# A mixture-of-experts layer: first blocks of small experts in two passes, sums of halves under conditions, weight remainders on VectorE alone

## The chip, the cores and the metric

One core of one Trainium2 chip. The metric is the device time of one execution in microseconds (us). TensorE does the matmuls, ScalarE (ACT in the profile) and VectorE (DVE) work on what they leave in PSUM, GpSimd (POOL) issues gathers and scatters, SyncE (SP) issues the loads of weights. Each engine runs its own instructions strictly in the order in which they are written to it, and waits on semaphores for the others.

## The reference

One decoder layer over 2048 tokens of width 1024: four sequence mixers, a norm, then a hierarchical mixture of experts, and a second norm. The change is in the experts alone. Each token goes to 2 of 32 experts, which lie in 4 groups of 8:

```
group_p, group_idx = lax.top_k(softmax(xt @ w_rg + b_rg), 1)
e_logits = (xt @ w_re + b_re).reshape(t_tok, 4, 8)[its group]
expert_p, local_idx = lax.top_k(softmax(e_logits), 2)
gate = group_p * expert_p / sum(expert_p)
def expert_block(xb, e):                 # rows of one expert
    return (silu(xb @ w_gate[e]) * (xb @ w_up[e])) @ w_down[e]
y = segment_sum(y_rows * gate, token)
```

`w_gate` and `w_up` are 1024 x 512 for each expert, `w_down` is 512 x 1024, all in float32. How many rows an expert has is known only at run time: 4096 assignments fall on 32 experts.

## The kernel before

**Precision.** A float32 product is made of matmuls on high and low parts: `xh*wh + xh*wl + xl*wh`, three passes. The high part of a weight is a cast on ScalarE (`split_piece`, L1835), the low part is what the cast loses, a subtraction on VectorE or GpSimd (L1836). The weights of one expert come in six raw pieces of 1 MB (`m_raw`, 5 buffers): four for gate and up (`m_g`, 8 buffers, just the high and low parts of one expert), two for down (`m_dh`, `m_dl`). So there are 12 casts and 12 subtractions of 128 x 1024 for each expert. Of the subtractions 8 are VectorE's, and 4 are GpSimd's: the last gate/up piece and the last down piece.

**Blocks.** The rows of an expert are gathered in blocks of 128: block 0 always, block 1 if the count is over 128, block 2 (rare) if it is over 256, in `third`. A block of full form is three passes: 48 matmuls of 128 x 512 for gate and up (`moe_gu`, L1884, into the PSUM tiles `m_g0` for block 0 and `m_g1` for block 1; the trace calls both `m_g`, the instruction lists `m_g_18058` and `m_g_18059`) and 24 for down (`moe_dn`, L1916, into `m_y`, the one tile `yb` for both blocks). A block with at most 64 rows can be done in two passes: its transposed rows are laid out `spread`, so that the high parts of 64 rows and the low parts of the same rows fill one 128-wide operand (`passes`). That is 32 and 16 matmuls; the sums of the two halves must then be added. For gate and up `fold` does that (two ScalarE copies scaled by the 0/1 mask `m_half`, L1892, and two VectorE adds, L1893), for down a multiply-add in `moe_y` (L1925). Before the change only block 1 has this form: TensorE chooses it by a condition, the other engines do the fold and the multiply-add for every expert, scaled by 0 where nothing is to be added.

**One turn.** The 32 experts are done one after the other, in the order `ORDER`. In the turn of expert e the kernel does gate and up of e, the activation (`moe_h`: a tanh on ScalarE, L1900, and two VectorE steps, L1901 and L1902, for each block), turns the gathered rows of e + 1 (`turned`: TensorE transposes into `bank`, L1408, a ScalarE cast L51 and a VectorE subtraction L52 per bank of 4 transposes; two PSUM banks in all), does down of e - 1 (`down0`, then `down1`), turns the activations `m_t` of e into `m_h`, and splits the next weights. After each down come two ScalarE copies of `m_y` (`moe_y`, L1923), and a scatter-add (L1930) by GpSimd. `down1` writes the tile that the copies of `down0` read.

**What sets the order.** The calls in `moe()` are a program; a scheduler then orders each engine's instructions inside the stretches between conditions. A condition (`tc.If`) is a boundary: what is inside a branch stays together, and what is outside can't be put between its instructions. All blocks 0 are outside any condition before the change. `third` is a condition that four engines test once in each turn (L2011).

## Time and profile before

| | |
|---|---|
| median of 3 runs | 3057.15 us (3054.57 to 3073.09) |
| profiled execution, its own time | 3065.59 us |
| its span, first to last instruction | 3063.8 us |
| TensorE busy in the span | 2826.6 us (92%) |
| VectorE, ScalarE, GpSimd busy | 1934.6, 1225.6, 887.9 us |
| mean granted clock of TensorE | 0.946 of 2.4 GHz |

The span is the profiled execution alone; the median is of other executions of the same program. Busy times are sums over a program with quite different stages, so the stage of the experts, from about 1990 to 2935 us, has to be read by itself.

### The profile page before, as it was taken

What the parts mean: (1) busy time and instruction counts of PE and PEld (TensorE: products, weight loads), DVE (VectorE), ACT (ScalarE), POOL (GpSimd) and SP (SyncE); (2) the same over time, 40 slices, a digit from 0 to 9 for tenths busy, and PEclk for the clock granted to TensorE, in tenths of its full rate; (3) what the DMA queues carried; (4) which work ended last, traced back from release to release, by engine and by line L of the source; (5) the groups of instructions that cost most, each with busy time, mean ns of one, the idle gap of its engine ahead of it and who ended that gap; (6) DMA issues with size and microseconds to landing.
All of it is one profiled execution on the core that took longest, in us unless ns stands there. A gap on an engine that the chain in (4) does not pass through costs nothing. (4 is left out here: it accounts for less than half of the span.)

```text
span 3063.8 us, 42798 instructions
## 1 busy us (share of the span) xinstructions
PE 2826.6 (92%) x15420; PEld 2225.7 (73%) x15421; DVE 1934.6 (63%) x4061; ACT 1225.6 (40%) x2003; POOL 887.9 (29%) x552
## 2 busy tenths in 40 slices
PE   8999999999989999999999999898899888999866
PEld 6898877777867766665577799776677767777644
DVE  6366365366555567776646735677677866667868
ACT  4222132222124423333311112265576656566854
POOL 1000000011010023334431101445464544546524
PEclk9999999999989898989999999999999999999988
DMA  6332242121125422110243412377597767877865
GB/s 189 100 102 71 69 125 70 55 73 56 53 50 164 158 79 80 50 38 18 83 141 136 143 69 70 114 276 259 182 309 233 251 230 230 264 246 244 286 223 195
DMA packets 287042, 442.98 MB, mean 145 GB/s; under 512 B 84088, under 2 KB 152040, under 8 KB 286760
## 3 DMA queue, kind: packets, MB, share of 16 engines
q1 hardware_dynamic: 272200, 397.78, 39.2%
q0 software_dynamic: 14560, 41.47, 5.4%
q8 instruction: 172, 2.82, 0.4%
q14 instruction: 110, 0.90, 0.1%
HBM read 350.52 MB, written 96.50 MB: 146 GB/s over the span
## 5 line engine op out<-in xcount | busy, mean ns | idle before, releaser
L1884 PE MATMUL m_g<-m_g,xhl 128*128 128x512 f32 x2032 | 521.0, 404 | 16.4 <-PEq L2011 9.1
L1884 PEld LDWEIGHTS m_g<-m_g,xhl 128*128 128x128 f32 x2032 | 376.0, 192 | 110.1 <-issue 31.5
L1836 DVE TENSOR_TENSOR m_g<-m_raw,m_g 128x1024 fp32r<-128x1024 f32 x188 | 273.5, 1482 | 109.7 <-ACT m_g L1835 104.4
L1835 ACT CAST m_g<-m_raw 128x1024 fp32r<-128x1024 f32 x252 | 255.4, 1058 | 111.2 <-PEq L2011 99.2
L1916 PE MATMUL m_y<-m_dh,m_h 128*128 128x512 f32 x656 | 225.8, 409 | 24.0 <-PEq L2011 7.3
L59 PE MATMUL pbank<-xh,wh 128*128 128x512 f32 x544 | 226.6, 417 | 6.6 <-DVE us L213 3.6
L60 PE MATMUL pbank<-xl,wh 128*128 128x512 f32 x544 | 218.8, 402 | 0.0
L61 PE MATMUL pbank<-xh,wl 128*128 128x512 f32 x544 | 218.3, 402 | 0.0
L51 ACT CAST xhl<-bank 128x512 fp32r<-128x512 f32 x204 | 118.3, 609 | 240.2 <-PE bank L1408 239.1
L1836 POOL TENSOR_TENSOR m_g<-m_raw,m_g 128x1024 fp32r<-128x1024 f32 x64 | 184.9, 2971 | 84.5 <-ACT m_g L1835 47.5
L1466 PE MATMUL wide<-wt,xhl 128*128 128x512 f32 x768 | 183.2, 397 | 3.6 <-ACT xhl L51 3.6
L1836 POOL TENSOR_TENSOR m_dl<-m_raw,m_dh 128x1024 fp32r<-128x1024 f32 x64 | 178.3, 2819 | 23.9 <-ACT m_dh L1835 23.7
L1304 POOL TENSOR_TENSOR mla_acc<-mla_acc,mla_pt 128x512 f32<-128x512 f32 (+3 forms) x112 | 132.2, 1180 | 147.4 <-ACT mla_pt L1302 137.4
L1466 PEld LDWEIGHTS wide<-wt,xhl 128*128 128x128 f32 x768 | 143.9, 189 | 40.0 <-ACT xhl L51 7.5
L1302 ACT ACTIVATE mla_pt<-sbank 128x512 f32<-128x512 f32 (+3 forms) x160 | 85.3, 533 | 212.6 <-PE sbank L1298 110.8
L1916 PEld LDWEIGHTS m_y<-m_dh,m_h 128*128 128x128 f32 x656 | 128.6, 196 | 57.1 <-issue 10.8
L52 DVE TENSOR_TENSOR xhl<-bank,xhl 128x512 fp32r<-128x512 f32 x204 | 136.2, 684 | 49.9 <-ACT xhl L51 48.0
L1930 POOL DMA_INDIRECT accd<-m_y,m_put x47 | 96.1, 2044 | 247.2 <-ACT m_y L1923 148.1
L59 PE MATMUL pbank<-wh,xh 128*128 128x256 f32 x512 | 151.8, 296 | 0.0
L1646 PE MATMUL gate<-wt,xhl 128*128 128x354 f32 (+1 forms) x864 | 150.3, 331 | 1.1 <-ACT xhl L51 0.9
L60 PE MATMUL pbank<-wl,xh 128*128 128x256 f32 x512 | 150.3, 293 | 0.0
L61 PE MATMUL pbank<-wh,xl 128*128 128x256 f32 x512 | 149.1, 291 | 0.0
(643 smaller groups left out, 6279.6 us busy)
## 6 DMA issues: line engine op xcount, KB each, us to landing
m_raw<-in_moe_w_down SPq DMA_DIRECT2D x64, 1024.0 KB
m_raw<-in_moe_w_gate SPq DMA_DIRECT2D x126, 512.0 KB
m_raw<-in_moe_w_up SPq DMA_DIRECT2D x126, 512.0 KB
wraw<-in_w_in SPq DMA_DIRECT2D x80, 256.0 KB
o_x<-in_x SPq DMA_DIRECT2D x16, 512.0 KB
x1d<-m_g SPq DMA_DIRECT2D x16, 512.0 KB
accd<-wide SPq DMA_DIRECT2D x16, 512.0 KB
m_raw<-accd SPq DMA_DIRECT2D x7, 1024.0 KB
```

The source lines that it names most:

```text
L51: nc.scalar.copy(hi, src)
L52: (eng and nc.gpsimd or nc.vector).tensor_sub(lo, src, hi.bitcast(F32))
L59: nc.tensor.matmul(out, lh, rh, start=start, stop=False)
L60: nc.tensor.matmul(out, lh, rl, start=False, stop=False)
L61: nc.tensor.matmul(out, ll, rh, start=False, stop=stop)
L1304: (nc.vector if kt in self.SUMS else nc.gpsimd).tensor_add(acc[:, c0 * 128:512], acc[:, c0 * 128:512], pt[:, 0:n])
L1466: nc.tensor.matmul(p[:, j], a[:, k], W[k][bb][:, j * 512:j * 512 + 512], start=k == 0 and i == 0, stop=k == 7 and i == 2)
L1646: nc.tensor.matmul(p[:, 0:n], a[:, k], b[:, o:o + n], start=k == 0 and i == 0, stop=k == 7 and i == 2)
L1835: self.nc.scalar.copy(h[:, i], raw[:, i])
L1836: lo_eng.tensor_sub(l[:, i], raw[:, i], h[:, i].bitcast(F32))
L1884: self.mark["pe"] = self.nc.tensor.matmul(banks[:, j], a, b[:, k % 2, j * 512:j * 512 + 512], start=k == 0 and i == 0, stop=k == 7 and i = ...
L1916: self.nc.tensor.matmul(p[:, j], a, b[:, k % 2, j * 512:j * 512 + 512], start=k == 0 and i == 0, stop=k == 3 and i == len(ps) - 1)
```

## The change

First blocks get the form that second blocks had: their rows and activations are turned `spread` too, and TensorE tests whether the count is at most 64 (`sized(e, 0, ...)`), for gate/up and for down. The masked fold and the masked multiply-add of the down sums give way to a fold without a mask, inside a condition that ScalarE and VectorE test, for gate/up and down, for both blocks; the condition for block 1 is a pair, over 128 first and then at most 192. ScalarE and VectorE now load the counts into registers for it. The 4 subtractions of each expert that GpSimd did go to VectorE.

```diff
--- before.py
+++ after.py
@@ -1733,7 +1733,7 @@
             self.lists(lt)
             self.moe_gather(self.midx[:, 0:1], x0)
             embed(L + 2)
-            return G0, self.turned(x0)
+            return G0, self.turned(x0, spread=True)
 
     LATE = 4
 
@@ -1770,8 +1770,7 @@
         half, u = tl([128, n], F32, "m_half"), tl([128, n], F32, "m_mu")
         self.mhalf = half
         v = half.rearrange("p (e b) -> p b e", e=32)
-        nc.vector.memset(half, 1.0)
-        for b in range(1, self.NB):
+        for b in range(self.NB):
             nc.vector.tensor_scalar(v[:, b], self.base, 128.0 * b + 64, None, op0=OP.is_le)
 
         plain = tl([128, n], F32, "m_plain")
@@ -1884,12 +1883,15 @@
                     self.mark["pe"] = self.nc.tensor.matmul(banks[:, j], a, b[:, k % 2, j * 512:j * 512 + 512],
                                           start=k == 0 and i == 0, stop=k == 7 and i == len(ps) - 1)
 
-    def fold(self, p, m):
+    def fold(self, p, m=None):
 
         t = self.mw.tile([128, 512], F32, name="m_fold", bufs=1)
         for j in range(2):
             h = t[64 * j:64 * j + 64]
-            self.nc.scalar.activation(h, p[64:128, j], AF.Identity, scale=m[64:128])
+            if m is None:
+                self.nc.scalar.copy(h, p[64:128, j])
+            else:
+                self.nc.scalar.activation(h, p[64:128, j], AF.Identity, scale=m[64:128])
             self.nc.vector.tensor_add(p[0:64, j], p[0:64, j], h)
 
     def moe_h(self, banks, gate, t=None):
@@ -1964,11 +1966,11 @@
         def load_g(e):
             done = list(G0) if e == 0 else []
             R = [self.raw_gu(e, k) for k in range(len(done), 4)]
-            GW[e] = done + [self.split_piece((self.g_tile(), self.g_tile()), r, nc.gpsimd if i == len(R) - 1 else nc.vector) for i, r in enumerate(R)]
+            GW[e] = done + [self.split_piece((self.g_tile(), self.g_tile()), r, nc.vector) for r in R]
 
         def load_d(e):
             R = [self.raw_dn(e, k) for k in range(2)]
-            DW[e] = [self.split_piece(self.d_tiles(), r, g) for r, g in zip(R, (nc.vector, nc.gpsimd))]
+            DW[e] = [self.split_piece(self.d_tiles(), r, nc.vector) for r in R]
 
         def gather0(e):
             if e < experts:
@@ -1986,25 +1988,39 @@
                 self.moe_put(Y.pop(e), put(e, 1))
 
         def turn(e, b):
-            return self.moe_ht(H.pop((e, b)), spread=b > 0)
-
-        def sized(e, b, f):
-
-            with tc.If(cnt[e, "pe"] > 128 * b + 64) as c:
-                f(False)
-            with c.Else():
-                f(True)
+            return self.moe_ht(H.pop((e, b)), spread=True)
+
+        def sized(e, b, f=None, p=None):
+
+            def pe():
+                with tc.If(cnt[e, "pe"] > 128 * b + 64) as c:
+                    f(False)
+                with c.Else():
+                    f(True)
+
+            def add():
+                with tc.If(cnt[e, "two"] <= 128 * b + 64):
+                    self.fold(p)
+
+            g, n = (pe, "pe") if f else (add, "two")
+            if b:
+                with tc.If(cnt[e, n] > 128 * b):
+                    g()
+            else:
+                g()
 
         yb = self.yb
 
+        def down(e, b, h):
+            sized(e, b, lambda s: self.moe_dn(h, DW[e], yb, half=s))
+            sized(e, b, p=yb)
+            return self.moe_y(yb)
+
         def down0(e, h):
-            self.moe_dn(h, DW[e], yb)
-            self.moe_put(self.moe_y(yb), put(e, 0))
+            self.moe_put(down(e, 0, h), put(e, 0))
 
         def down1(e, h):
-            with tc.If(cnt[e, "pe"] > 128):
-                sized(e, 1, lambda s: self.moe_dn(h, DW[e], yb, half=s))
-            Y[e] = self.moe_y(yb, half(e, 1))
+            Y[e] = down(e, 1, h)
 
         def third(e):
 
@@ -2029,7 +2045,7 @@
 
         def counts(e):
             if e % 4 == 0:
-                for t, k, g in ((self.turn_cnt, "pe", [ET.PE]), (self.turn_cnt, "pool", [ET.Pool]), (self.turn_max, "four", FOUR)):
+                for t, k, g in ((self.turn_cnt, "pe", [ET.PE]), (self.turn_cnt, "pool", [ET.Pool]), (self.turn_cnt, "two", [ET.Activation, ET.DVE]), (self.turn_max, "four", FOUR)):
                     for i, v in enumerate(load_counts(t, e, g)):
                         cnt[e + i, k] = v
 
@@ -2038,7 +2054,7 @@
         if not x0:
             gather0(0)
         gather(0)
-        x0 = x0 or self.turned(X[0])
+        x0 = x0 or self.turned(X[0], spread=True)
         x1 = self.turned(X[1], spread=True)
         b0, b1 = self.gu
         ht = None
@@ -2049,14 +2065,13 @@
             third(e - 1)
             gather(e + 1)
             gather0(e + 1)
-            self.moe_gu(x0, GW[e], b0)
-            with tc.If(cnt[e, "pe"] > 128):
-                sized(e, 1, lambda s: self.moe_gu(x1, GW[e], b1, half=s))
-            H[e, 0] = self.moe_h(b0, gate(e, 0))
-            self.fold(b1, half(e, 1))
-            H[e, 1] = self.moe_h(b1, gate(e, 1))
+            sized(e, 0, lambda s: self.moe_gu(x0, GW[e], b0, half=s))
+            sized(e, 1, lambda s: self.moe_gu(x1, GW[e], b1, half=s))
+            for b, p in enumerate((b0, b1)):
+                sized(e, b, p=p)
+                H[e, b] = self.moe_h(p, gate(e, b))
             if e + 1 < experts:
-                x0 = self.turned(X[0])
+                x0 = self.turned(X[0], spread=True)
                 load_g(e + 1)
             if e == 31:
                 self.lx, self.lp, self.lt = {}, {}, {}
```

With the conditions the scheduler gives the engines another order. Three places, all in the turn of an expert in the middle of the stage; in brackets stand the semaphores that an instruction waits for, named by the engine that raises them.

TensorE, from the end of `down0` to the start of `down1`, before: `m_y<-` are the down matmuls, `m_t` the turning of the activations, `m_g_18058` gate and up of the next expert's block 0.

```order
L1916 MATMUL m_y<-m_dl,m_h 128x512
L1916 MATMUL m_y<-m_dh,m_h 128x512
L1408 MATMUL bank<-ident,m_t 128x128 [waits DVE_49]
L1408 MATMUL bank<-ident,m_t 128x128 x3
L1884 MATMUL m_g_18058<-m_g,xhl 128x512 [waits Activation_49]
L1884 MATMUL m_g_18058<-m_g,xhl 128x512 x4
L2005 COMPARE_AND_BRANCH
L1993 COMPARE_AND_BRANCH
L1916 MATMUL m_y<-m_dh,m_h 128x512 [waits Activation_49]
```

And in the changed kernel, where `xg_18064` is the turning of the next expert's rows of block 0:

```order
L1996 UNCONDITIONAL_BRANCH
L1408 MATMUL bank<-ident,m_xg_18064 128x128 [waits DMASW4_49,PE_49]
L1408 MATMUL bank<-ident,m_xg_18064 128x128 x3
L1408 MATMUL bank<-ident,m_xg_18064 128x128 [waits PE_49]
L1408 MATMUL bank<-ident,m_xg_18064 128x128 x3
L2002 UNCONDITIONAL_BRANCH
L2007 UNCONDITIONAL_BRANCH
L2002 UNCONDITIONAL_BRANCH
L2007 COMPARE_AND_BRANCH
L1996 COMPARE_AND_BRANCH
L1918 MATMUL m_y<-m_dh,m_h 128x512 [waits DVE_49,Activation_49]
```

Before, the rows of the next expert are turned at the start of `down0`, and `down0`, the first bank of `m_t` and five gate/up matmuls stand between that and `down1`; now the eight transposes of the rows come after `down0`, `down1` comes right behind them, then both banks of `m_t`, and the gate/up matmuls of the next expert in one piece behind those.

ScalarE, at the start of the same turn, before: `m_t<-m_g_18058` is the tanh of block 0, `xhl<-bank` the cast of the turned rows, `m_y<-m_y` the copies after `down0`.

```order
L1835 CAST m_g<-m_raw 128x1024 [waits DMAHW7_49,DMAHW0_49,PE_49]
L1900 ACTIVATE m_t<-m_g_18058 128x512
L1892 ACTIVATE m_fold<-m_g_18059,m_half 64x512 [waits DVE_49,Activation_49]
L51 CAST xhl<-bank 128x4x128 [waits PE_49] x2
L1835 CAST m_g<-m_raw 128x1024
L1892 ACTIVATE m_fold<-m_g_18059,m_half 64x512 [waits DVE_49]
L1835 CAST m_g<-m_raw 128x1024 [waits DMAHW2_49,DMAHW1_49]
L1835 CAST m_g<-m_raw 128x1024
L1900 ACTIVATE m_t<-m_g_18059 128x512 [waits DVE_49]
L1923 COPY m_y<-m_y 128x512 [waits DMASW5_49,PE_49]
L1923 COPY m_y<-m_y 128x512
```

And in the changed kernel, without the branches' bodies:

```order
L1834 CAST m_g<-m_raw 128x1024 [waits DMAHW7_49,DMAHW0_49,PE_49]
L1834 CAST m_g<-m_raw 128x1024
L51 CAST xhl<-bank 128x4x2x64 [waits DVE_49,PE_49,Activation_49]
L2002 COMPARE_AND_BRANCH
...
L2007 COMPARE_AND_BRANCH
...
L1902 ACTIVATE m_t<-m_g_18058 128x512 [waits DVE_49]
L1902 ACTIVATE m_t<-m_g_18059 128x512 [waits DVE_49]
L51 CAST xhl<-bank 128x4x2x64 [waits PE_49]
L1834 CAST m_g<-m_raw 128x1024 [waits DMAHW2_49,DMAHW1_49]
L1834 CAST m_g<-m_raw 128x1024
L2002 COMPARE_AND_BRANCH
...
L1925 COPY m_y<-m_y 128x512 [waits DMASW6_49,DVE_49]
```

The tanh of block 0 stood ahead of the casts of the turned rows; now it stands behind the first of them and behind the two conditions for gate/up, and the copies of `m_y` stand behind both tanh, the second cast of the rows, two casts of weights and a third condition.

VectorE, at the same place, before: L1901 and L1902 are the steps after the tanh, `xhl<-bank` the low parts of the turned rows.

```order
L1836 TENSOR_TENSOR m_g<-m_raw,m_g 128x1024 [waits DMAHW0_49,DVE_49,DMAHW7_49,PE_49,Activation_49]
L1901 SCALAR_TENSOR_TENSOR m_t<-m_t,m_g_18058 128x512 [waits Activation_49]
L1893 TENSOR_TENSOR m_g_18059<-m_g_18059,m_fold 64x512 [waits Activation_49]
L1902 SCALAR_TENSOR_TENSOR m_t<-m_t,m_gate,m_g_18058 128x512 [waits DVE_49]
L52 TENSOR_TENSOR xhl<-bank,xhl 128x4x128 [waits Activation_49]
L1893 TENSOR_TENSOR m_g_18059<-m_g_18059,m_fold 64x512 [waits Activation_49]
L52 TENSOR_TENSOR xhl<-bank,xhl 128x4x128 [waits PE_49]
L1836 TENSOR_TENSOR m_g<-m_raw,m_g 128x1024
```

And in the changed kernel:

```order
L1835 TENSOR_TENSOR m_g<-m_raw,m_g 128x1024 [waits Activation_49]
...
L1903 SCALAR_TENSOR_TENSOR m_t<-m_t,m_g_18059 128x512 [waits Activation_49]
L1904 SCALAR_TENSOR_TENSOR m_t<-m_t,m_gate,m_g_18058 128x512 [waits DVE_49]
L1904 SCALAR_TENSOR_TENSOR m_t<-m_t,m_gate,m_g_18059 128x512 [waits DVE_49]
L2002 COMPARE_AND_BRANCH
L1895 TENSOR_TENSOR m_y<-m_y,m_fold 64x512 [waits PE_49,Activation_49]
L1895 TENSOR_TENSOR m_y<-m_y,m_fold 64x512 [waits Activation_49]
L2002 UNCONDITIONAL_BRANCH
L2002 UNCONDITIONAL_BRANCH [waits DVE_49]
L52 TENSOR_TENSOR xhl<-bank,xhl 128x4x2x64 [waits PE_49]
```

The low parts of the turned rows, which free the two PSUM banks for `m_t`, now come behind all four steps of both blocks and behind the condition for the down sums.

## Rows read from the trace of the kernel before

**Rows 1.** Busy by stretch: length, PE, PEld, DVE, ACT, POOL, granted clock, DMA share, GB/s

```profile
1990.00:2935.00 945.00, 846.47 (x3847) 670.72 (x3846) 677.54 (x708) 609.54 (x822) 490.98 (x215) 0.96 0.77 253
```

**Rows 2.** The page's costliest groups: count, busy us, mean ns, idle before

```profile
L1884 PE MATMUL m_g<-m_g,xhl 128*128 128x512 f32 x2032 | 521.0, 404 | 16.4 <-PEq L2011 9.1
...
L1836 DVE TENSOR_TENSOR m_g<-m_raw,m_g 128x1024 fp32r<-128x1024 f32 x188 | 273.5, 1482 | 109.7 <-ACT m_g L1835 104.4
...
L1836 POOL TENSOR_TENSOR m_g<-m_raw,m_g 128x1024 fp32r<-128x1024 f32 x64 | 184.9, 2971 | 84.5 <-ACT m_g L1835 47.5
...
L1930 POOL DMA_INDIRECT accd<-m_y,m_put x47 | 96.1, 2044 | 247.2 <-ACT m_y L1923 148.1
```

**Rows 3.** Waits of TensorE in the 32 turns: us in total, times, longest

```profile
PE bank L1408 <- DVE m_t L1902: 14.9, 10, 2.4
PE bank L1408 <- DVE m_h L52: 11.3, 4, 4.2
...
PE m_y L1916 <- ACT m_y L1923: 6.2, 6, 2.4
```

**Rows 4.** Timeline of TensorE in turns 13 and 14: start, us, what

```profile
2396.88 1.03 PE L1408 MATMUL bank<-ident,m_xg 128*128 128x128 f32 x8
...
2417.68 1.06 PE L1408 MATMUL bank<-ident,m_xg 128*128 128x128 f32 x8 [0.45 <-PEq L2011]
...
2424.64 0.60 PE L1408 MATMUL bank<-ident,m_t 128*128 128x128 f32 x4
...
2428.07 0.63 PE L1408 MATMUL bank<-ident,m_t 128*128 128x128 f32 x4 [2.36 <-DVE m_t L1902]
...
2429.70 0.40 PE L1916 MATMUL m_y<-m_dh,m_h 128*128 128x512 f32 x1
```

**Rows 5.** Timeline of TensorE, a longer run of matmuls

```profile
2286.93 15.03 PE L1884 MATMUL m_g<-m_g,xhl 128*128 128x512 f32 x65
```

**Rows 6.** Timeline of ScalarE in the same turn

```profile
2418.12 0.69 ACT L1892 ACTIVATE m_fold<-m_g,m_half 64x512 f32<-64x512 f32 x1 [0.26 <-ACTq L2011]
...
2420.62 1.07 ACT L51 CAST xhl<-bank 128x512 fp32r<-128x512 f32 x2
2421.72 2.00 ACT L1835 CAST m_g<-m_raw 128x1024 fp32r<-128x1024 f32 x2
2423.62 0.59 ACT L1900 ACTIVATE m_t<-m_g 128x512 f32<-128x512 f32 x1
...
2426.94 1.07 ACT L1923 COPY m_y<-m_y 128x512 f32<-128x512 f32 x2
```

**Rows 7.** Timeline of VectorE in the same turn

```profile
2418.84 0.69 DVE L1893 TENSOR_TENSOR m_g<-m_g,m_fold 64x512 f32<-64x512 f32 x1 [0.26 <-ACT m_fold L1892]
...
2423.11 1.29 DVE L52 TENSOR_TENSOR xhl<-bank,xhl 128x512 fp32r<-128x512 f32 x2
...
2425.45 0.68 DVE L1901 SCALAR_TENSOR_TENSOR m_t<-m_t,m_g 128x512 f32<-128x512 f32 x1
...
2427.18 0.74 DVE L1902 SCALAR_TENSOR_TENSOR m_t<-m_t,m_gate,m_g 128x512 f32<-128x512 f32 x1
...
2449.00 1.23 DVE L1836 TENSOR_TENSOR m_g<-m_raw,m_g 128x1024 fp32r<-128x1024 f32 x1 [0.47 <-DVEq L2011]
```

**Rows 8.** Timelines of VectorE and GpSimd, one subtraction against two

```profile
2441.66 6.88 DVE L1836 TENSOR_TENSOR m_dl<-m_raw,m_dh 128x1024 fp32r<-128x1024 f32 x1
...
2442.19 5.25 POOL L1836 TENSOR_TENSOR m_dl<-m_raw,m_dh 128x1024 fp32r<-128x1024 f32 x2
```

**Rows 9.** Timeline of TensorE around an idle stretch

```profile
2269.83 0.76 PE L1916 MATMUL m_y<-m_dh,m_h 128*128 128x512 f32 x1 [4.14 <-PEq L2011]
2270.39 1.91 PE L1408 MATMUL bank<-ident,m_xg 128*128 128x128 f32 x8
...
2273.17 0.39 PE L1916 MATMUL m_y<-m_dl,m_h 128*128 128x512 f32 x1
```

## The prediction

> **What bounds the kernel now.** I read the stage of the experts first by stretches: of 945 us TensorE is busy 846, VectorE 678, ScalarE 610, GpSimd 491 [rows 1]. So the stage runs at TensorE's pace. Its matmuls are pipelined, so the mean of 404 ns overstates their price; 65 in a row took 15.03 us, 0.231 each [rows 2, 5].
>
> Next come the counts, since the change acts on blocks of at most 64 rows. Routing the reference's inputs through its own formulas gives, in the order of the turns: 43, 154, 142, 89, 96, 308, 191, 99, 86, 109, 240, 186, 51, 147, 124, 103, 69, 289, 89, 186, 49, 129, 198, 188, 42, 256, 38, 79, 30, 72, 102, 112. The trace agrees: 47 scatters are 32 first blocks, 13 over 128 rows and 2 over 256; 2032 gate/up matmuls are 32 x 48 + 5 x 48 + 8 x 32 [rows 2], so 5 second blocks are full and 8 are half. Six first blocks have at most 64 rows: turns 0, 12, 20, 24, 26, 28.
>
> Then the timeline of one turn, to see how TensorE stays busy while a value goes round the other engines. Turn 14: rows turned at 2417.68, under `down0`; first `m_t` bank at 2424.64; second at 2428.07 after a wait of 2.36; `down1` at 2429.70 [rows 4]. Between these lie gate/up matmuls of the next expert, which need nothing new. That filling is why TensorE waits so little: in the whole stage 14.9 us for the activations, 11.3 for a bank at VectorE's `m_h` step and 6.2 for the copies of `m_y`, together 32.4 [rows 3]. The chain of waits of the whole program ends in the norms behind the stage; everything ahead of them shifts it one for one.
>
> **The change part by part.**
>
> *Matmuls taken out.* 16 + 8 in each of 6 turns: 144 x 0.231 = 33.3 us. Not all counts: gate/up of 32 matmuls uses up a weight piece in 8 x 0.231 = 1.85 us, while VectorE needs 2 x 1.23 = 2.46 to subtract one [rows 7], so three pieces come 0.6 late in each of these turns: 6 x 1.8 = 11 lost. **-22**.
>
> *The order.* This is the part that decides. All gate/up and all down matmuls now lie inside conditions, so nothing can be put between them, and nothing of them between other things. The order lists show the consequence for every turn: `down0`, eight transposes, then `down1` or at once `m_t`. Walk it from the end of `down0`. The first four transposes take 0.60, as those of `m_t` [rows 4]. ScalarE is in order, and its next instruction is the cast of that bank, ahead of the tanh: half of 1.07. Two conditions not taken follow; behind one such condition ScalarE lost 0.26 [rows 6]: 0.52. Tanh of block 0: 0.59.
>
> - Turns in which `down1` is skipped: VectorE does 0.68 + 0.68 + 0.74 + 0.74, a condition not taken (0.47 lost in front of an instruction behind one), and the low part of the turned rows, half of 1.29 [rows 7]. Only then is a bank free for `m_t`. Sum 0.60 + 0.54 + 0.52 + 0.59 + 2.84 + 0.47 + 0.65 = 6.2; TensorE is busy with transposes for 1.06 of it, and nothing else may come ahead. It stands 5.15 us.
> - Turns with `down1`: it waits for the copies of `m_y`. ScalarE goes on with the second tanh 0.59, the second cast 0.54, two weight casts 2.00, a condition 0.26, the copies 1.07 [rows 6]. Sum 6.7, less 1.06: TensorE stands 5.65 us.
>
> 31 turns have the chain: 18 x 5.15 + 13 x 5.65 = 166. The waits of [rows 3] are the same links where they were still covered, and go: -32.4. **+134**.
>
> *Folds in conditions.* A fold is copy, add, copy, add, each waiting for the one ahead: 2 x (0.69 + 0.69) = 2.76 [rows 6, 7]. Before, every expert had one for gate/up, but with other work between its steps. Now a gate/up fold stands ahead of the tanh in 6 + 8 turns: 38.6. A down fold of a small first block stands on VectorE ahead of the turned rows: 6 x 2.76 = 16.6. A down fold of a half second block delays only weights; 0 to 2 us in 8 turns, I take 8 in all, since gate/up has two pieces ready. **+63**. What is dropped in return (copies and adds scaled by 0, the multiply-adds of `m_y`) was off TensorE's path and gives nothing.
>
> *The clock.* After 4.14 us of idling a run of eight transposes took 1.91 instead of 1.06; from 2269.83 to 2273.17 four matmuls and these transposes needed 3.34 instead of 1.06 + 4 x 0.231 = 1.98 [rows 4, 9]: the lower of the two clock levels for a while, 1.36 lost. If each new stop costs that: 31 x 1.36 = 42, less some 8 that the waits that go had cost: **+34**.
>
> *Subtractions moved.* 128 of them at 1.23 on VectorE instead of 2.97 on GpSimd [rows 2, 7]. VectorE's own cost falls too: one subtraction took 6.88 us while GpSimd's two (5.25) ran [rows 8]; 188 with a mean of 1.48 [rows 2] would come to 1.23. VectorE has then, in a turn without second block, 12 x 1.23 + 6 x 0.65 + 2 x 1.42 + 4 x 0.47 = 23.4 us, below the 29.5 of a mean turn [rows 1], and below 20.8 + 5.15 with the new stop. What this frees on TensorE's path is the 11.3 us already counted. The Trainium skill ("SBUF — State Buffer", section "Who interferes with whom") says that a VectorE instruction with two SBUF inputs and a GpSimd one that reads SBUF exclude each other for the whole instruction. The 6.88 us agree with that. By this rule the removal of GpSimd's reads speaks for the change; it makes the gain of the first rival below, and no term here.
>
> *The rest.* Spread rows, one more comparison of 128 x 32, the count registers: 0 to 10. Down weights whose subtraction comes behind the last turned rows: 0 to 18. New jumps on TensorE, two in a turn, 0 to 0.45 each as in front of [rows 4]: 0 to 28. I take 0, because long runs with a jump in them show no gap [rows 5].
>
> Sum: -22 + 134 + 63 + 34 = +209 on 3065.6, so 3274.6 for the profiled execution. That execution lay 8.4 above the median of the runs: **3266 us**.
>
> **The rivals.**
>
> 1. *Faster: VectorE's relief decides.* If ScalarE and VectorE run so far ahead that the chain stays covered, the waits of [rows 3], the matmuls and the half-speed stretches go and nothing comes: 3057 - 32 - 33 - 8 = 2984. For it: VectorE loses up to 5.6 us to one collision [rows 8]. Against it: the order lists put the tanh behind a cast that can't start before `down0` ends. It decides where the new stop costs under 73/31 = 2.4 us a turn.
> 2. *VectorE becomes the bound, nothing else happens.* A turn without second block or `down1` takes as little as 20.8 us now, 2396.88 to 2417.68 [rows 4]; with VectorE's 23.4 it can't be under that. At most 18 x 2.6 = 47 come, against 22 of matmuls and 32 of waits: 3050, within 1%. Against it: it needs TensorE's chain covered as well.
> 3. *The same mechanism at its low end.* Links overlap (starts follow at 0.5 to 0.6 where I took durations), 4.1 us instead of 5.4 on the mean, folds and clock hidden: 3266 - 40 - 63 - 34 = 3129.
> 4. *Jumps that miss.* TensorE's 4.14 us of idling followed its way past a skipped second block and `third` [rows 9]. If each of the 62 new jumps cost as much, 257 come on top: 3523. Against it: most skips of second blocks show 0.45 or less, as in [rows 4]. The Trainium skill ("Runtime: NRT & Kernel Launch", section "Instruction fetch mechanics") says that a taken branch whose target lies outside the pages held must be fetched before execution goes on; the idle stretch would fit it, the small gaps show that short jumps stay inside.
>
> **How the numbers follow.** Chances: forecast with all between its ends 0.81, rival 1 0.09, rival 2 0.06, rival 4 0.04. A measurement tells about 1% (31 us) from no change. Low end: rival 3, 3129. High end: the three "0 to" items and 8 more of folds, 64 on top: 3330. With a little on that side the range is 3130 to 3340, which leaves out rivals 1, 2 and 4. Slower 0.85, within 1% 0.06, faster 0.09.
>
> **What would show it.** TensorE waiting at L1408 (`m_t`) for VectorE in turns without `down1`, and at the first down matmul for ScalarE's copies in turns with it, near 5 us each, some 160 us in the stage. The granted clock of the stage falls below 0.96. Turns of small experts show 2.8 us more ahead of the tanh. VectorE's 1024-wide subtractions come at 1.23, none over 2. The forecast is wrong if those two waits sum to less than 75 us, or if TensorE's gaps stand elsewhere: at the gate/up matmuls waiting for weights (VectorE too full) or in front of conditions with nothing to wait for (jumps).

## The result, and the profile of the kernel after

The changed kernel takes 3353.51 us (median; 3351.36 to 3355.27), the kernel before in the same comparison 3057.32. The ratio is 1.0965, with a 95% interval of 1.0934 to 1.0995. So the change costs 296 us where 209 were forecast, and the time lies above the range. The profiled execution took 3351.36 us (span 3349.6); against the 3065.6 of the one before that is 285.8 more.

First the stretches. Up to 1990 us the two timelines lie within 6 us of each other; the stage of the experts ended near 2935 before [rows 1] and ends near 3220 now. The view by stretches of the kernel after (busy time and number of instructions by engine, granted clock, DMA share, GB/s):

```profile
1990.00:3220.00 1230.00, 889.42 (x3680) 717.86 (x3680) 677.24 (x757) 594.57 (x808) 129.71 (x88) 0.85 0.59 192
```

The stage is 1230 us instead of 945, 285 more, which is the whole difference but for those 6 us. TensorE is busy 43 us more although 144 matmuls are gone, and idle 340.6 instead of 98.5. The clock fell from 0.96 to 0.85. VectorE's busy time is what it was. So the engine that set the pace now stands, and runs slower between its stops.

Then TensorE's waits in that stretch, by the line that waits and what ended the wait (sum in us, times, longest):

```profile
PE bank L1408 <- DVE xhl L52: 98.3, 17, 9.7
PE m_y L1918 <- ACT m_y L1925: 54.4, 8, 8.5
PE m_y L1918 <- DVEq L2027: 45.5, 11, 5.2
PE m_y L1918 <- ACTq L2002: 38.5, 5, 8.5
PE m_y L1918 <- PEq L2027: 28.0, 14, 6.5
PE bank L1408 <- DVEq L2007: 20.1, 3, 7.9
PE bank L1408 <- DVE m_t L1904: 12.3, 1, 12.3
```

They answer to [rows 3], where 14.9 was the largest. The rows of L1408 (the transposes of `m_t`) sum to 130.7, and the two of L1918 that ScalarE ends (the second blocks' down) to 92.9: 223.6 us at the two places that the prediction named. The two rows with L2027 are others: the first blocks' down matmuls, just behind the condition of `third`.

The timeline of TensorE shows the two kinds of stop in one turn (start, length, engine, line, what, number; in brackets the idle time before and what ended it):

```profile
2585.83 0.93 PE L1408 MATMUL bank<-ident,m_xg 128*128 128x128 f32 x7
2591.88 0.57 PE L1918 MATMUL m_y<-m_dh,m_h 128*128 128x512 f32 x1 [5.12 <-PEq L2027]
...
2599.01 1.03 PE L1408 MATMUL bank<-ident,m_xg 128*128 128x128 f32 x8
2604.78 1.97 PE L1408 MATMUL bank<-ident,m_t 128*128 128x128 f32 x8 [4.74 <-DVEq L2007]
2606.40 12.46 PE L1883 MATMUL m_g<-m_g,xhl 128*128 128x512 f32 x48
2618.70 1.04 PE L1408 MATMUL bank<-ident,m_xg 128*128 128x128 f32 x8
2623.74 0.76 PE L1918 MATMUL m_y<-m_dh,m_h 128*128 128x512 f32 x1 [4.01 <-DVEq L2027]
```

At 2604.78 is the forecast stop: rows turned at 2599.01, and nothing to do until a bank is free. It is 4.74 where 5.15 was worked out. At 2591.88 and 2623.74 TensorE stands ahead of the first block's down. Where a second block ran, that stop is 0.6 to 0.7 us; in the 17 turns with neither a second block's gate/up nor a third block ahead it is 4.0 to 6.5, 75 us in all (the last of them lies just behind 3220). The eight transposes at 2604.78 took 1.97, the half-speed price of [rows 9].

What ScalarE and VectorE do at these two places, from their timelines:

```profile
2599.70 0.61 ACT L51 CAST xhl<-bank 128x512 fp32r<-128x512 f32 x1 [6.28 <-issue]
2600.66 1.08 ACT L1902 ACTIVATE m_t<-m_g 128x512 f32<-128x512 f32 x2 [0.35 <-ACTq L2007]
...
2622.90 1.99 ACT L1834 CAST m_g<-m_raw 128x1024 fp32r<-128x1024 f32 x2 [2.42 <-PEq L2027]
```
```profile
2589.36 1.22 DVE L1835 TENSOR_TENSOR m_dl<-m_raw,m_dh 128x1024 fp32r<-128x1024 f32 x1
...
2601.29 1.28 DVE L1903 SCALAR_TENSOR_TENSOR m_t<-m_t,m_g 128x512 f32<-128x512 f32 x2 [7.56 <-ACT m_t L1902]
2602.49 1.40 DVE L1904 SCALAR_TENSOR_TENSOR m_t<-m_t,m_gate,m_g 128x512 f32<-128x512 f32 x2
2604.04 1.53 DVE L52 TENSOR_TENSOR xhl<-bank,xhl 128x512 fp32r<-128x512 f32 x2
...
2619.98 1.29 DVE L52 TENSOR_TENSOR xhl<-bank,xhl 128x512 fp32r<-128x512 f32 x2 [3.00 <-ACT xhl L51]
2621.18 2.35 DVE L1835 TENSOR_TENSOR m_dl<-m_raw,m_dh 128x1024 fp32r<-128x1024 f32 x2
```

The chain to `m_t` reads as in the prediction: cast, conditions passed, tanh, four steps of VectorE, the low part of the rows. At the other stop two things end together. VectorE's last two subtractions of down weights stand behind the low part of the next second block's rows and end at 2623.53. And ScalarE goes on at 2622.90, let go by TensorE's sequencer, which had needed until then to pass L2027 though its last transposes ended at 2619.74. Which of the two makes this stop the trace doesn't tell. In the one that ends at 2591.88 VectorE's last subtraction was done at 2590.58, 1.3 us earlier, so there it isn't VectorE alone. The last experiments tell the two apart.

The subtractions themselves came out as forecast. The costliest groups of L1835 in the stage (count, busy, mean ns), against a mean of 1482 in [rows 2]:

```profile
L1835 DVE TENSOR_TENSOR m_g<-m_raw,m_g 128x1024 fp32r<-128x1024 f32 x247 | 288.3, 1220 | 94.5 <-ACT m_g L1834 68.4 <-DVEq L2007 9.8 <-DMA m_raw<-in_moe_w_down 6.2
L1835 DVE TENSOR_TENSOR m_dl<-m_raw,m_dh 128x1024 fp32r<-128x1024 f32 x124 | 146.3, 1215 | 0.7 <-ACT m_dh L1834 0.7
```

### The profile page after: what moved, and what is told of

Read it like the earlier page. It is cut to its first block, busy times and chain, and to the rows that moved or that the text cites. A ratio compares the mean times of both kernels' runs of the same rounds, so it can differ in the third digit from the quotient of the medians.

```text
span 3349.6 us, 42999 instructions
## 1 busy us (share of the span) xinstructions
PE 2866.4 (86%) x15276; PEld 2271.3 (68%) x15277; DVE 1942.4 (58%) x4117; ACT 1215.3 (36%) x1995; POOL 517.7 (15%) x424
## 5 line engine op out<-in xcount | busy, mean ns | idle before, releaser
L1883 PE MATMUL m_g<-m_g,xhl 128*128 128x512 f32 x1936 | 484.5, 411 | 10.1 <-DVE xhl L52 8.7
L1883 PEld LDWEIGHTS m_g<-m_g,xhl 128*128 128x128 f32 x1936 | 383.8, 201 | 97.0 <-ACT xhl L51 8.2
L1918 PE MATMUL m_y<-m_dh,m_h 128*128 128x512 f32 x608 | 256.2, 484 | 192.3 <-ACT m_y L1925 54.4
L1835 DVE TENSOR_TENSOR m_g<-m_raw,m_g 128x1024 fp32r<-128x1024 f32 x252 | 294.1, 1220 | 94.6 <-ACT m_g L1834 68.5
L1918 PEld LDWEIGHTS m_y<-m_dh,m_h 128*128 128x128 f32 x608 | 146.9, 242 | 239.7 <-issue 60.9
L1918 PE MATMUL m_y<-m_dl,m_h 128*128 128x512 f32 x360 | 171.6, 477 | 0.0
L1408 PE MATMUL bank<-ident,m_t 128*128 128x128 f32 x264 | 52.2, 359 | 131.0 <-DVE xhl L52 97.2
L1839 POOL DMA_INDIRECT m_xg<-x1d,m_idx x46 | 46.2, 1005 | 718.6 <-PEq L2007 361.7
L1932 POOL DMA_INDIRECT accd<-m_y,m_put x47 | 89.4, 1902 | 436.3 <-ACT m_y L1925 188.0
L1835 DVE TENSOR_TENSOR m_dl<-m_raw,m_dh 128x1024 fp32r<-128x1024 f32 x128 | 150.9, 1215 | 0.9 <-ACT m_dh L1834 0.9
```

The lines of the kernel that those rows point to most:

```text
L1835: lo_eng.tensor_sub(l[:, i], raw[:, i], h[:, i].bitcast(F32))
L1883: self.mark["pe"] = self.nc.tensor.matmul(banks[:, j], a, b[:, k % 2, j * 512:j * 512 + 512], start=k == 0 and i == 0, stop=k == 7 and i = ...
L1918: self.nc.tensor.matmul(p[:, j], a, b[:, k % 2, j * 512:j * 512 + 512], start=k == 0 and i == 0, stop=k == 3 and i == len(ps) - 1)
```

## The experiments

The theories. **A**, the prediction's: first blocks' matmuls stand in conditions, so nothing fills TensorE's waits. **B**: the subtractions moved to VectorE make the down weights late. **C**: the conditions on ScalarE and VectorE do it, wherever the matmuls stand. **J**: TensorE's jumps past skipped code take time of their own, since instructions have to be fetched.

**1. Subtractions alone** (`e1_sub_only`, the kernel before with)

```diff
-[self.split_piece(..., nc.gpsimd if i == len(R) - 1 else nc.vector) for i, r in enumerate(R)]
+[self.split_piece(..., nc.vector) for r in R]
-DW[e] = [self.split_piece(self.d_tiles(), r, g) for r, g in zip(R, (nc.vector, nc.gpsimd))]
+DW[e] = [self.split_piece(self.d_tiles(), r, nc.vector) for r in R]
```

> The kernel before with all subtractions for trailing weights on VectorE and nothing else of the change. Theory A (what costs time is that the matmuls of first blocks now stand inside conditions, so that nothing fills TensorE's waits): the blocks are as before, so the subtractions alone are worth between nothing and a small gain, 3010 to 3060 us; TensorE's waits at m_t stay under 30 us. Theory B (the subtractions moved to VectorE make the down weights late; this is the stop of some 4 us ahead of the first block's down matmuls that the changed kernel has in each turn without a second block, 77 us in all): that stop appears here too, 18 x 3 to 4 us = 50 to 75 and half-speed stretches behind it, so 3110 to 3150 us.

Measured: 3079.82 us, ratio 1.0085 (1.0059 to 1.0111). Between the two. Of its waits in the stage, that of B is there, and that at `m_t` is small:

```profile
PE m_y L1916 <- DVEq L2011: 39.9, 12, 3.8
...
PE bank L1408 <- DVE m_t L1902: 8.5, 7, 1.5
```

In the turn whose stop ends at 2092.71, VectorE's last subtraction of down weights ends at 2092.50, while TensorE's sequencer had let ScalarE go at 2091.17. So B is a real stop, but the subtractions cost some 26 us in this order of work, not 296.

**2. All but the subtractions** (`e2_no_sub`): the changed kernel with the two lines of experiment 1 turned back.

> The changed kernel, but GpSimd keeps its four subtractions per expert. Theory A: the stops at m_t (131 us in the changed kernel) and at the second blocks' down matmuls (93) stay as they are; the time stays within 1% of the changed kernel, 3330 to 3390 us, the upper half because VectorE and GpSimd get in each other's way again. Theory B: the stop ahead of the first blocks' down matmuls falls from 77 us to under 30, with some 20 to 40 of half speed, so 3260 to 3300 us. A rival to B (TensorE's jump past the skipped second block and third makes that stop): it stays at 70 to 80 us.

Measured: 3483.6 us, ratio 1.1398 (1.1353 to 1.1444), 130 us above the changed kernel. All theories missed this. Its waits, and its subtractions by engine:

```profile
PE bank L1408 <- DVE m_t L1904: 187.0, 26, 12.2
PE bank L1408 <- DVE m_h L52: 89.8, 22, 7.7
```
```profile
L1835 POOL TENSOR_TENSOR m_dl<-m_raw,m_dh 128x1024 fp32r<-128x1024 f32 x61 | 158.1, 2612 | 290.5 <-ACT m_dh L1834 282.9 <-ACTq L2027 7.6
L1835 DVE TENSOR_TENSOR m_dl<-m_raw,m_dh 128x1024 fp32r<-128x1024 f32 x62 | 137.4, 2228 | 10.1 <-ACT m_dh L1834 10.1
```

VectorE's down subtractions take 2.23 us on the mean beside GpSimd's, 1.22 alone, and the wait at the low parts of `m_h` (89.8) is one that the changed kernel doesn't have. In the changed order these durations lie on TensorE's path; before, such waits came to 11.3 [rows 3]. So moving the subtractions to VectorE pays in the changed order, while in the old one (experiment 1) it cost.

**3. First blocks as before** (`e3_first_full`): the changed kernel, but first blocks take the full passes outside conditions.

```diff
-            sized(e, 0, lambda s: self.moe_gu(x0, GW[e], b0, half=s))
+            self.moe_gu(x0, GW[e], b0)
...
-            sized(e, b, lambda s: self.moe_dn(h, DW[e], yb, half=s))
-            sized(e, b, p=yb)
+            if b:
+                ...
+            else:
+                self.moe_dn(h, DW[e], yb)
```

> The changed kernel, but first blocks always take the full passes, as before: no condition and no fold for them. The folds of second blocks in conditions and VectorE's subtractions stay. 144 matmuls more than the changed kernel (+33 us). Theory A: the transposes stand between matmuls again, the waits at m_t and at the second blocks' down matmuls fall from 224 us to under 70; with 8 folds of gate/up ahead of tanh (22 us) the time is 3060 to 3150 us. Rival C (the conditions on ScalarE and VectorE make the stops, by their order and their passing time, wherever the matmuls stand): second blocks have theirs still, so at least half of the 296 us stays, 3200 us or more. Theory B: the stop ahead of the first blocks' down matmuls stays near 77 us.

Measured: 3055.95 us, ratio 0.9982 (0.9951 to 1.0013). Everything comes back, although TensorE does 33 us of matmuls more than in the changed kernel. Its waits in the stage:

```profile
PE m_y L1919 <- DVEq L2031: 23.5, 7, 4.1
PE bank L1408 <- DVE m_h L52: 18.2, 14, 1.9
...
PE bank L1408 <- DVE xhl L52: 5.7, 8, 1.1
```

The stops at `m_t` are gone, that ahead of the first down is a third of its size. A holds, C loses: the second blocks' conditions on ScalarE and VectorE are all there.

**4. No conditions on ScalarE and VectorE** (`e4_masked`)

```diff
-            sized(e, b, p=yb)
-            return self.moe_y(yb)
+            return self.moe_y(yb, half(e, b))
...
-                sized(e, b, p=p)
+                self.fold(p, half(e, b))
```

> The changed kernel, with its conditions for TensorE on first blocks, but no conditions for ScalarE and VectorE: folds are unconditional, scaled by 0 or 1, as second blocks had them before. Theory A, with the price per link: matmuls stand in whole blocks still, and m_t still ahead of the next gate/up block, so a stop at m_t stays in all 31 turns, without the two conditions and conditional folds some 4.2 us each = 130 us; down of second blocks comes behind the next gate/up block and its stop (93 us) goes. Idle time falls by some 95 us and the clock's share by 30 to 40: 3200 to 3240 us. Rival C: with the conditions on ScalarE and VectorE gone nearly everything returns, 3060 to 3120 us, m_t waits under 40 us. If the jumps of TensorE were the cost, nothing returns: 3330 us or more.

Measured: 3633.17 us, ratio 1.1880 (1.1833 to 1.1927): 280 us above the changed kernel. C falls, and so does the size that A gave. Its two largest waits, and TensorE's timeline in one turn:

```profile
PE bank L1408 <- DVE m_t L1904: 396.0, 61, 7.6
PE m_y L1918 <- DVEq L2026: 132.0, 17, 8.8
```
```profile
2405.90 1.04 PE L1408 MATMUL bank<-ident,m_xg 128*128 128x128 f32 x8
2414.30 1.08 PE L1408 MATMUL bank<-ident,m_t 128*128 128x128 f32 x4 [7.37 <-DVE m_t L1904]
2421.16 1.08 PE L1408 MATMUL bank<-ident,m_t 128*128 128x128 f32 x4 [5.77 <-DVE m_t L1904]
```

Masked folds (a copy of 0.68 and an add of 0.69, twice a block) are steps of the chain now, in every turn, and weight casts and subtractions get between them: the `m_t` of either block is waited for by itself, and the stop ahead of the first down is 7.7 to 8.8 us in each of 17 turns (132.0). VectorE isn't full: it is busy 823 of 1510 us. The masked folds of second blocks stood in the kernel before too, with gate/up matmuls to cover them; now they cost time, since that cover is gone. The second blocks' down no longer waits, as expected, but that is less than what came.

**5. Conditional folds of second blocks alone** (`e5_cond_folds`): `e3_first_full` with the subtractions turned back as in experiment 2.

> The kernel before with one part of the change alone: the sums of halves of second blocks stand in conditions (and moe_y's multiply-adds with them); first blocks and subtractions as before. If the parts add up, this is worth what tells e3_first_full from e1_sub_only, 3056 - 3080 = -24 us: 3036 us, ratio 0.992. If conditional folds in TensorE's chain cost as they did in the changed kernel (8 small second blocks at 2.76, or TensorE's waits at m_t growing), it is 3060 to 3080 us.

Measured: 3110.77 us, ratio 1.0119 (1.0065 to 1.0173). The parts don't add up: conditional folds alone cost 1.2%, VectorE's subtractions alone 0.85%, both together (`e3_first_full`) nothing. The trace shows where this kernel loses: TensorE's transposes wait 60.2 us for the low parts of `m_h` (11.3 in [rows 3], 18.2 in `e3_first_full`), and VectorE's subtractions for gate/up are at 1.76 us on the mean, beside GpSimd's, where `e3_first_full` has 1.22.

```profile
L1408 PE MATMUL bank<-ident,m_xg 128*128 128x128 f32 x512 | 80.2, 293 | 66.3 <-DVE m_h L52 60.2 <-DVEq L2039 3.1 <-PEq L2033 1.9
L1836 DVE TENSOR_TENSOR m_g<-m_raw,m_g 128x1024 fp32r<-128x1024 f32 x186 | 319.9, 1764 | 110.6 <-ACTq L2003 44.2 <-ACTq L2008 43.5 <-ACT m_g L1835 17.4
```

**6. and 7. One of the two blocks** (`e6_gu_cond`: conditions on first blocks' gate/up alone; `e7_dn_cond`: on their down alone). The edits are those of experiment 3, one each, and the index list for the rows of the full passes.

> The changed kernel, but the first blocks' down multiplication is always full and outside conditions (the index list for its rows follows); gate/up of first blocks in conditions as in the change. Theory A says that either block alone leaves room: transposes of the next rows come ahead of 24 down matmuls (5.5 us) that cover most of the 6.2 us from the transposes to m_t. So the stop at m_t is 1 to 3 us a turn instead of 5 and more, down matmuls wait little for weights since they come a run of transposes later: 96 matmuls less than with full blocks (-22 us), 3050 to 3120 us. If a block of gate/up matmuls in a condition is enough for the whole loss, 3250 us or more.

> The changed kernel, but the first blocks' gate/up is always full and outside conditions; their down multiplication in conditions as in the change, its fold too. Theory A: gate/up matmuls can stand between transposes and waits again, so the stops at m_t are under 40 us in all and those at the second blocks' down matmuls gone; 48 matmuls less than with full blocks (-11 us), 6 folds ahead of the turned rows (up to +17): 3045 to 3090 us. If a condition around down is enough for the whole loss, 3250 us or more.

Measured: 3190.43 us, 1.0389 (1.0324 to 1.0453), and 3210.71 us, 1.0429 (1.0360 to 1.0499). Both above A's numbers. The waits of the two (first `e6_gu_cond`, then `e7_dn_cond`) show what A had left out:

```profile
PE m_y L1925 <- DVEq L2037: 32.6, 7, 5.1
PE m_y L1925 <- ACT m_y L1932: 30.3, 13, 3.6
PE bank L1408 <- DVE xhl L52: 26.2, 18, 3.0
PE m_y L1925 <- ACT m_g L1841: 20.2, 5, 4.2
```
```profile
PE m_y L1927 <- DVEq L2036: 59.1, 14, 5.1
...
PE bank L1408 <- DVE xhl L52: 10.1, 9, 3.4
```

At `m_t` A is right: 26.2 and 10.1 where the changed kernel has 98.3. But the stop of 4 to 5 us ahead of the first down is there in full in either; most of these stops end with VectorE passing the condition of `third` (L2037, L2036).

**8. Down subtractions earlier** (`e8_d_first`, the changed kernel with)

```diff
+            load_d(e)
             if e + 1 < experts:
                 x1 = self.turned(X[1], spread=True)
-            load_d(e)
```

> The changed kernel with load_d one step earlier in the program, ahead of the next second block's turned rows, so that VectorE's four subtractions of down weights stand ahead of the low parts of those rows, which wait for TensorE's end of gate/up. If the stop of some 4 us ahead of the first blocks' down matmuls (77 us in all) comes from subtractions standing behind that wait, it falls under 25 us, and with half speed behind it the time is 3260 to 3300 us. If it comes from TensorE's jumps past skipped blocks, it stays and the time is within 1% of the changed kernel, 3330 us or more.

Measured: 3323.85 us, ratio 1.0841 (1.0765 to 1.0916), 1% below the changed kernel. The same kind of turn, TensorE and then VectorE:

```profile
2607.44 1.03 PE L1408 MATMUL bank<-ident,m_xg 128*128 128x128 f32 x8
2612.23 0.76 PE L1918 MATMUL m_y<-m_dh,m_h 128*128 128x512 f32 x1 [3.76 <-PEq L2027]
```
```profile
2602.80 4.63 DVE L1835 TENSOR_TENSOR m_dl<-m_raw,m_dh 128x1024 fp32r<-128x1024 f32 x4
2608.72 1.29 DVE L52 TENSOR_TENSOR xhl<-bank,xhl 128x512 fp32r<-128x512 f32 x2 [1.28 <-ACT xhl L51]
```

The subtractions end at 2607.43 and VectorE's rows at 2610.01, and still TensorE stands until 2612.23. The 17 stops fell only from 75 to 62 us. So there is a second cause of much the same length behind B. Between 2609 and 2610, in the middle of the stop, the DMA view has this row (packets, MB), and none of its kind in the us before:

```profile
q8 instruction: 1, 0.02, 6.8%
```

**9. and 10. The code that TensorE jumps over.** In a turn without a second block it jumps past 80 matmuls of that block's gate/up, then past 84 of `third` (transposes among them). `e9_short_third` is `e8_d_first` with `third` cut to 20, so the two experts that have a third block leave out some 80 matmuls, 18 us; `e10_long_third` makes it 204, none of the new ones executed:

```diff
-self.lean(h, DW[e], yb, 4, cnt[e, "pe"] > 320)
+self.lean(h, DW[e], yb, 1)
-self.lean(x, GW[e + 1], yb, 8, cnt[e + 1, "pe"] > 320)
+self.lean(x, GW[e + 1], yb, 1)
```
```diff
+                    with tc.If(one(e) > 1000):
+                        for _ in range(5):
+                            self.moe_dn(h, DW[e], yb)
```

> e8_d_first with 8 of the 72 and more matmuls of a third block left in the program (the rest of its sums is left out, for the two experts that have one: about 80 executed matmuls, 18 us). Every other turn only jumps over that stretch of code. In e8_d_first 67 us of stops ahead of the first blocks' down matmuls stayed, though VectorE's subtractions were done 2 to 5 us earlier; each goes with a fetch of 16 KB of instructions. If a fetch behind TensorE's jump past the third block makes these stops (theory J), a short stretch keeps the target within what is there: the stops fall under 30 us, 3324 - 18 - 40 - 15 (half speed) = 3250 us. If the jump past the skipped gate/up block makes them, or work of VectorE and ScalarE, they stay: 3305 us.

> e8_d_first with 120 matmuls more in the third block's code, in a condition that no expert meets: nothing of it is executed, only the stretch that TensorE jumps over is longer. Theory J: the 13 turns with a second block, whose stop ahead of the first block's down matmuls is 0.6 to 0.8 us in e8_d_first, get 2 to 3 us as well, +30 us and some half speed: 3350 to 3375 us; the others stay at about 4. If no fetch is involved: 3324 us within 0.5%, stops as in e8_d_first.

Measured: 3268.82 us, 1.0701 (1.0658 to 1.0744), and 3385.42 us, 1.1067 (1.1027 to 1.1108). The 17 stops sum to 45 us with the short code (under 30 were expected), 62 with the code as it is, 110 with the long one. A turn of each, short and then long:

```profile
2331.65 1.03 PE L1408 MATMUL bank<-ident,m_xg 128*128 128x128 f32 x8
2334.43 0.47 PE L1920 MATMUL m_y<-m_dh,m_h 128*128 128x512 f32 x1 [1.74 <-DVEq L2029]
```
```profile
2339.83 1.03 PE L1408 MATMUL bank<-ident,m_xg 128*128 128x128 f32 x8
2348.47 0.76 PE L1918 MATMUL m_y<-m_dh,m_h 128*128 128x512 f32 x1 [7.60 <-PEq L2027]
```

With the short code the stop ends with VectorE's low part of the rows (1.74, its floor in 9 of the 17); with the long one TensorE needs 7.6 to come past. J holds: the length of code that is only passed over sets the stop. That the time goes into fetching instructions is argued from the instruction queue. Over the whole program the pages list 168 packets of some 16 KB with the short code, 185 in `e8_d_first` and 216 with the long one, 31 more for code that never runs (short, as it is, long):

```profile
q8 instruction: 168, 2.75, 0.3%
q8 instruction: 185, 3.03, 0.4%
q8 instruction: 216, 3.54, 0.4%
```

J's detail was wrong: in experiment 10 the turns with a second block stay at 0.6 to 1.1 us all but once (2.5). There a row of 32 or 48 matmuls is under way ahead of `third`, which would hide the price of the jump; it is the turns in which TensorE jumps twice with only the eight transposes ahead that pay more. Three of the 17 stops are at 1.74 to 1.75 in experiment 8 too; why the same jump costs no more there isn't shown. Of the 55 us between experiments 8 and 9 some 18 are the matmuls left out and 17 the stops; the rest isn't taken apart.

**11. Experiments 3 and 8 together** (`e11_first_full_d_first`)

> e3_first_full with load_d ahead of the next second block's turned rows, as in e8_d_first. e3_first_full has 37 us of stops at the first blocks' down matmuls, most ended by VectorE. If its late subtractions of down weights make them, 20 to 25 of these go: 3056 - 25 = 3030 us, ratio 0.990, faster than the kernel before. If not, ratio 0.998 as e3_first_full, and the stops stay.

Measured: 3065.71 us, ratio 1.0017 (0.9997 to 1.0037). Nothing gained; the stops at L1919 ended by VectorE are 22.3 us (11 times) instead of 24.4 (8 times), and those ended by TensorE's own sequencer 7.9 instead of 1.7. B's cure doesn't help in this order. No version tried is faster than the kernel before by more than the noise.

**12. Conditions without short passes** (`e12_never_small`): the bound of first blocks set from 64 rows to 1.

> The changed kernel with the bound for first blocks at 1 row instead of 64: the conditions stand where they stand, on all three engines, but all 32 first blocks take the full passes and none is folded. By the prediction's terms the six small experts gave -22 us of matmuls and cost 6 x (2.76 + 2.76) = 33 us of folds, so the kernel without them is 11 us faster than the changed one: 3340 us, ratio 1.093. If what the change costs lies in the turns that use the short passes, 3250 us or less; if short passes do pay, 3365 us or more.

Measured: 3357.44 us, ratio 1.0960 (1.0920 to 1.1000), the changed kernel's own. The passes saved in six small experts and their folds pay each other off within 15 us. The whole loss is there without one short pass of a first block; with experiment 3, it comes with the conditions around the first blocks.

## Why the prediction was right in direction and wrong in size

The stage's 285 us, by the prediction's own terms:

- *The order and the folds*: +134 and +63, 197 in all. Measured at the two places named: 223.6, less the 32.4 of [rows 3] that went: +191. Right, and most single stops too: 4.7 to 5.2 for 5.15 at `m_t` without a fold, 5.4 to 5.6 for 5.65 at the second blocks' down, 8.0 to 8.5 with a fold. One stop of 12.3, in the first turn, is longer than anything worked out. Experiment 3 shows the cause, experiments 6 and 7 that the stops at `m_t` take both blocks, experiment 4 what it costs when more steps of ScalarE and VectorE come into the chain.
- *Matmuls taken out*: -22 with their late weights. It is 33 by count: the 11 us of late weights didn't come, the idle time ahead of gate/up matmuls fell in the stage, from 16.3 to 10.0 us. Experiment 12 fits folds that ate it: without short passes the time is the same.
- *The clock*: +34 forecast. TensorE's busy time rose by 43 us where 33 should have gone: +76. Mis-sized, in part because there were 48 longer stops (31 + 17) and not 31; at 1.36 each, less the 8, that is 57. The other 19 are not taken apart.
- *The rest*, taken as 0: this is the step that failed. What is left of TensorE's added idle time is 242 - 191 = +51. The first blocks' down matmuls stand 77.5 us in the stage (45.5, 28.0 and one stop of 4.0 that ScalarE ends), where the same places had some 8 before; other stops fell by 18. The prediction had two of its causes in hand and priced both too low. "Down weights whose subtraction comes behind the last turned rows: 0 to 18" is B, about 4 us in each of 17 turns. "New jumps: 0, because long runs with a jump in them show no gap [rows 5]" is J: those rows were of jumps with matmuls still under way, and the new places have only eight transposes. Either cause would make nearly the whole stop, which is why taking out one (experiment 8) gave 30 us. For J alone experiment 8 shows it; for B alone it is read from VectorE's end at 2623.53, 0.2 us ahead of TensorE, and no run had the short code in the old order.

Sum: 191 + 51 - 33 + 76 = 285. Forecast: 197 + 0 - 22 + 34 = 209. Neither the 51 nor the clock's 42 too few would have left the range by itself; together they did.

Of the rivals, 1 to 3 did not come. Rival 4's mechanism is there, but at 17 places, not 62, and beside another cause. Its row was read rightly: in the kernel before, the 4.14 us of [rows 9] hold a fetch of instructions as well (16 KB on the same queue between 2265 and 2266), and ScalarE is let go by TensorE's sequencer at 2269.51, 0.3 us before its end; GpSimd's down subtractions end there too, so that row has both causes as well. The Trainium skill ("Runtime: NRT & Kernel Launch", section "Instruction fetch mechanics") says that a taken branch to code that isn't held must fetch first. Experiments 8 to 10 agree: in the turns shown the stop is 1.74 us with the short code, where VectorE ends it, 3.8 with the code as it is and 7.6 with the long one. Where matmuls are under way the price is hidden, 0.6 to 1.1 us.

VectorE's subtractions came to 1.22 us as forecast. That this would be worth 130 us inside the changed kernel was not seen: the prediction asked what GpSimd's reads cost in the old order, where TensorE was covered. The Trainium skill ("SBUF — State Buffer", section "Who interferes with whom") says that a VectorE instruction with two SBUF inputs contends with a GpSimd one that reads SBUF; experiment 2 agrees, with 2.23 us beside GpSimd's subtractions against 1.22 alone.

Still open: the 19 us of clock; and why in the order of `e3_first_full` VectorE's subtractions bring less of B's stop (24.4 us) than in experiment 1 (39.9), so that together with the conditional folds nothing is lost.

## What to carry to other kernels

A condition around a block of matmuls takes more than its comparison: nothing can be moved into the block or out of it, so every chain through other engines that those matmuls covered shows in full. Before putting one in, list what stands between its neighbours in the order of the engine, and price each gap by the whole chain and by the jump with nothing under way. When an edit that should cure a stop gives only a small part of it, look for a second cause of the same length beside it before dropping the theory.

## What was not expected of the hardware

A jump shows or doesn't by what is under way: in experiment 10 TensorE passes code of 204 matmuls within 0.6 to 1.1 us behind a second block's matmuls, while in experiment 8 jumps past 80 and 84 with only transposes ahead make stops of 3.5 to 6.2 us in the 8 turns where its own sequencer ends them. Instructions that are never executed cost 61 us in experiment 10. And moving the same four subtractions of an expert to VectorE costs 26 us in one order of work (experiment 1) and gives 130 in another (experiment 2).
